# Nine quads by seven products in each last sweep, in turns with plain ones, and side work held one item earlier

## The chip, the core and the metric

The kernel runs on one core of one Trainium2 chip (trn2). The metric is the device time of one launch in microseconds (us), the median of several runs.

## The reference

One layer of a hybrid decoder block on x (256 rows, 2048 columns), all in f32. What touches the change is its second half:

```python
x = x + g1 * (merged @ w_o[l])
h2 = modulate(rms_norm(x, norm2_g[l]), sh2, sc2)
gate, up = jnp.split(h2 @ w_ffn_in[l], 2, axis=-1)
x = x + g2 * ((jax.nn.silu(gate) * up) @ w_ffn_out[l])
return rms_norm(x, final_g)
```

The six modulation rows (shift, scale and gate, twice) are `silu(c) @ ada_w + ada_b`. The hidden width of the FFN is 5632, which is 44 tiles of 128 for `w_ffn_out`.

## The kernel before, in words

**Products in f32.** Each f32 operand is split into a high and a low half. ScalarE (ACT) rounds the high half (`hi`, L330), VectorE (DVE) subtracts it (`lo`, L342), and TensorE (PE) makes a product from three matmuls: high by high, low by high, high by low. Weights stream from memory through SyncE's queue (SP) as tiles `raw` (L313). Half of a weight tile is 512 columns wide, a whole one 1024.

**Items.** The program is a list `items`, one per weight tile. For item i, `step` issues the load of item i+6, the derived tile ("made") of item i+5, the `hi` of item i+4 and the `lo` of item i+3, then what hangs on the item's `before` list, then its matmuls, and it lets the work that waits (posts and sides) into the order of DVE and ACT when a planner's clocks for these engines leave room. The order on every engine is fixed when the program is built.

**Quads by seven products.** A quad is two k tiles (2 x 128) by two column blocks (2 x 512) for two row tiles. A plain quad is two items of 12 matmuls: 8 products of three matmuls. `seven` makes the same from 7 products by sums of weights and of activations (Strassen's scheme in Winograd's form): 21 matmuls in four items. The first item is a half tile (product p, 3 matmuls), the second a whole one (6). The third is `wx`, a difference that GpSimd's queue (POOL) builds by two loads and two adding loads (L443, L447); it gives r and u. The fourth is `wy`, made by DVE from `wx` and two raw tiles (L458, L459); it gives q and the last product. The sums of the activations stand ready as `fs`; ACT rounds them (`ah`, L1404) and DVE subtracts (`al`, L1409), once per seven. The products p, q, r and u of all sevens of a sweep gather in four PSUM banks `pp`, `pq`, `pr`, `pu`, and `combined` (L1425 on) adds them up once at the sweep's end: eleven DVE operations of 512 columns.

**FFN.** `w_ffn_in` is read in eleven slabs. Slab 0 is plain, the others run by `add_pair` with four quads by seven products of eight. `up_f_post` or `gated_rows` transposes the result of a slab (`ft{s}`, two PSUM banks), and `f_parts` makes from it the high and low halves (`fh`, `fl`, L988 and L991) for plain quads, or the sums `fs` for the quads named in `SEVEN` (L1239 to L1249).

**Last sweeps.** `w_ffn_out` runs in two sweeps over k, one for each half of the output columns. The first 36 k tiles are 18 quads, in the order that `TURNS` writes out ("-" plain, "7" by seven products). The last 8 k tiles (the rest) are plain in sweep 1; in sweep 2 they come from two tensors of another layout (f2b, f2c), and behind them stand the products `late`, the last columns of the second row tile. `blocks` adds the residual: `y` (L1461) and `x` (L1463) on DVE, a square on ACT. For sweep 1 this happens at the start of sweep 2, for sweep 2 at the end, and then the final norm (`finish_first`, `finish_last`) scales and stores the rows.

**Side work.** The modulation rows are made by DVE between other work: one operation per column pair, `aw` (L532). `ada_to(m, n)` makes sure that the loads of columns are issued up to a point. `hold_sides` sets the planner's slack so low that no more of them are let in until the second norm (`second_norm`, L1101 on) sets it again.

The lines that the change touches before: `SEVEN` (L68), `TURNS` (L75), `load_rows` (L1048 to L1055) and `hold_sides` with its place (L1087 to L1092). In the changed kernel the lines from L1052 on are numbered two lower, from L1087 on one lower.

Of the kernel before, what the change touches and what calls it, by code (L numbers as in the profile page):

```python
# [64 lines left out]
N_MADE, N_HOLD = 5, 4  # L65

N_SUM = (16, 11)
SEVEN = tuple(range(6, 36, 4))  # L68

SEVEN_1, SLAB_7 = (4, 6, 10, 12), 1  # L70

SLAB_G = 4
TURNS_1 = {1: "---7-77-"}

TURNS = "--7-7-7-7-7-7-7-7-"  # L75
EARLY = NH - 2 * N_HOLD

N_SPARE = 5
# [5 lines left out]
def hybrid_layer(  # L84
# [21 lines left out]
    def b4(name, dt=F32, shape=(4, S)):  # L106
        used["b4"] += 1
        return bp.tile([P, *shape], dt, tag="b4", name=name)
# [6 lines left out]
    def sum_bank(name):  # L115
        return ps.tile([P, 512], F32, tag="bank", name=name)
# [178 lines left out]
    items = []  # L295
# [397 lines left out]
    for i in range(N_PIECES):  # L693
        for n in range(N_F if i == 0 else 0, len(START)):
            s, k0, k1 = START[n], ends[i][n], ends[i + 1][n]
# [8 lines left out]
    def ada_to(*ms):  # L704
        while not {(m, kt) for m in ms for kt in range(NK)} <= cols_done:
            if not ada.advance():
                clock["pe"] += 1
                halves.fetch()
# [339 lines left out]
    def load_rows(s):  # L1048
        def before():
            xr.append(b4(f"xr{s}", F32, (2, 512)))  # L1050
            nc.sync.dma_start(xr[s], x_r[:, s * 512:(s + 1) * 512].rearrange("(t p) n -> p t n", p=P))
            if s == 3:  # L1052
                ada_to(3, 4)
        return before

    def keep_rows(s):
# [29 lines left out]

    def hold_sides():  # L1087

        clock["slack"] = -1e9
        return 0, 0  # L1090

    items[-2].before.append(hold_sides)  # L1092

    def turn(p, of_w=False):

# [132 lines left out]
    def f_parts(s, pts):  # L1228

        seven_ = [j for j in range(2) if 4 * s + 2 * j in SEVEN]  # L1230
        if not seven_:
# [123 lines left out]
    def bank(t, n):  # L1355

        if (t, n) not in fin:
            fin[t, n] = sum_bank(f"pf{t}{n}")
        return fin[t, n]
# [39 lines left out]
    def seven_last(k, n, src):  # L1399
        parts = {}  # L1400

        def parts_high():
            hi = parts[0] = b4(f"ah{n}_{k}", F32R, (8, P))
            nc.scalar.copy(hi[:, 0:7, :], f_sum[k][:, 0:7, :])  # L1404
            return 0, 0.9

        def parts_low():
            lo = parts[1] = b4(f"al{n}_{k}", F32R, (8, P))
            nc.vector.tensor_tensor(lo[:, 0:7, :], f_sum[k][:, 0:7, :], f32(parts[0][:, 0:7, :]), op=ALU.subtract)  # L1409
            return 1.0, 0  # L1410

        def own(to):
            if to not in "pqru":
                return bank(int(to[0]), n + int(to[1]))
            if k == SEVEN[0]:
                fin[to] = sum_bank(f"p{to}{n}")
            return fin[to]

        items[-3].before.append(parts_high)
        items[-2].before.append(parts_low)  # L1420
        seven(
            (src[k], src[k + 1]), lambda j, i: src[k + j][:, i * 512:(i + 1) * 512], True,
            lambda a: [parts[h][:, a, :] for h in range(2)], own, k == SEVEN[0], k == SEVEN[-1],
            (lambda: combined(n)) if k == SEVEN[-1] else None,
        )  # L1425

    def combined(n):

        v = [b4(f"v{n}{i}", F32, (2, 512)) for i in range(2)]
        pq, pqu, pqr, pqur = v[0][:, 0, :], v[0][:, 1, :], v[1][:, 0, :], v[1][:, 1, :]  # L1430
        nc.scalar.copy(pq, fin["p"])

        def add(t, j, x):
            y = sp.tile([P, 512], F32, tag="t2", name=f"yv{n}{t}{j}")
            x2 = x2_of(t, (n + j) * 512, (n + j + 1) * 512)
            nc.vector.tensor_tensor(y, x, g2_of((n + j) * 512, (n + j + 1) * 512), op=ALU.mult)
            nc.vector.tensor_tensor(x2, y, x2, op=ALU.add)

        yield 0, 0.6
        add(0, 0, pq)  # L1440
        nc.vector.tensor_tensor(pq, fin["q"], pq, op=ALU.add)
        yield 1.8, 0
        nc.vector.tensor_tensor(pqu, fin["u"], pq, op=ALU.add)
        nc.vector.tensor_tensor(pqr, fin["r"], pq, op=ALU.subtract)
        nc.vector.tensor_tensor(pqur, fin["r"], pqu, op=ALU.subtract)
        yield 1.8, 0
        add(0, 1, pqr)
        yield 1.2, 0
        add(1, 0, pqu)
        yield 1.2, 0  # L1450
        add(1, 1, pqur)
        free(b4=2)
        yield 1.2, 0
        if n == 2:
            yield from early_rows()
# [38 lines left out]
    for n, src in ((0, w_f2a), (2, w_f2d)):  # L1494
        start = len(items)
        kinds = {"7": iter(SEVEN), "-": iter(k for k in range(0, EARLY, 2) if k not in SEVEN)}
        turns = [next(kinds[c]) for c in TURNS]
        for k in turns + list(range(EARLY, NH if n == 0 else EARLY, 2)):
            if k in SEVEN:
                seven_last(k, n, src)  # L1500
# [244 lines left out]
```

## Time and profile before

| | |
|---|---|
| median of 3 runs | 1537.02 us (1536.7 to 1537.57) |
| profiled execution | 1538.73 us, span 1537.0 us |
| TensorE clock granted | 0.998 |
| PE busy | 1521.0 us, 99% |
| DVE busy | 1365.3 us, 89% |
| ACT busy | 880.7 us, 57% |
| chain that ended last | PE 93%, DMA 3%, DVE 3% |

A row of the timeline gives the start and the length in us, the engine, the line, the operation with out<-in, and the count; in square brackets stands the idle time ahead of it on its engine and what ended it. Rows of one kind that follow each other are drawn together (x3). The spacing of two rows on one engine is a little shorter than the length of the first, since they overlap. "issue" is a wait for nothing that the profile shows.

### The profile page before, as it was taken

How to read it: one execution, taken by the hardware profiler on the slowest of the kernel's cores; microseconds unless marked ns; L12 is line 12 of the kernel's file. 1: busy time of each engine (PE TensorE's matmuls, PEld its weight loads, DVE VectorE, ACT ScalarE, POOL GpSimd, SP SyncE). 2: the span in 40 equal slices, each digit the busy share in tenths (PEclk: the TensorE clock that was granted, in tenths of full speed). 3: DMA queues.
4: the chain of work that ended last, by engine and by line, in shares of the span. 5: the costliest groups of instructions: out<-in, count | busy, mean ns of one | idle time of the engine just before them, and what ended most of it. 6: DMA issues, size and time to landing. Idle time of an engine off the chain costs nothing.

```text
span 1537.0 us, 20204 instructions
## 1 busy us (share of the span) xinstructions
PE 1521.0 (99%) x6851; PEld 1249.0 (81%) x6851; DVE 1365.3 (89%) x1835; ACT 880.7 (57%) x1142; POOL 163.5 (11%) x232
## 2 busy tenths in 40 slices
PE   8999999999999999999999999999999999999997
PEld 5788888888888787888887878888888888888886
DVE  7999999888898888988988899999999999888987
ACT  4654444886964446444444556656665556664664
POOL 0000000000000000000002231034212122321200
PEclk9999999999999999999999999999999999999999
DMA  9999988656786887999999999589898979989983
GB/s 368 383 345 362 345 315 301 207 181 217 241 286 226 291 308 283 364 325 341 377 373 347 312 338 273 167 254 332 274 273 248 269 243 298 288 257 297 275 266 124
DMA packets 138440, 444.58 MB, mean 289 GB/s; under 512 B 16064, under 2 KB 16224, under 8 KB 138336
## 3 DMA queue, kind: packets, MB, share of 16 engines
q1 hardware_dynamic: 113056, 384.02, 70.2%
q0 software_dynamic: 24992, 58.75, 16.1%
q8 instruction: 53, 0.87, 0.2%
q10 hardware_dynamic: 288, 0.52, 0.1%
q14 instruction: 51, 0.42, 0.1%
HBM read 439.02 MB, written 4.21 MB: 288 GB/s over the span
## 4 chain that ended last, share of the span: by engine, by line
PE 93%; DMA 3%; DVE 3%; ACT 0%; issue 0%; SPq 0%; DVEq 0%; ACTq 0%
PE pf L1391 10%; PE f L383 6%; PE f L382 6%; PE f L384 6%; PE wi L383 6%; PE wi L384 6%; PE wi L382 6%; PE wl L384 2%; PE wl L383 2%; PE wga L384 2%; PE wl L382 2%; PE wga L382 2%; PE wgl L383 2%; PE wga L383 2%; PE wgl L384 2%; PE wa L384 2%
## 5 line engine op out<-in xcount | busy, mean ns | idle before, releaser
L330 ACT CAST hi<-raw 128x1024 fp32r<-128x1024 f32 (+1 forms) x540 | 532.3, 996 | 419.1 <-PE wi L384 87.4
L342 DVE TENSOR_TENSOR lo<-raw,hi 128x1024 fp32r<-128x1024 f32 (+1 forms) x540 | 611.9, 1149 | 82.1 <-issue 37.7
L383 PE MATMUL wi<-lo,h 128*128 128x512 f32 x432 | 168.4, 390 | 3.3 <-DVE lo L342 3.3
L382 PE MATMUL wi<-hi,h 128*128 128x512 f32 x432 | 169.9, 393 | 0.0
L384 PE MATMUL wi<-hi,h 128*128 128x512 f32 x432 | 168.2, 389 | 0.0
L382 PE MATMUL f<-hi,h 128*128 128x512 f32 x406 | 158.8, 391 | 0.0
L383 PE MATMUL f<-lo,h 128*128 128x512 f32 x406 | 158.1, 389 | 0.0
L384 PE MATMUL f<-hi,h 128*128 128x512 f32 x406 | 158.0, 389 | 0.0
L532 DVE CUSTOM_DVE_ANT_0 aw<-aw,crow,vec 128x1024 f32<-128x1024 f32 x95 | 120.5, 1277 | 6.0 <-DMA aw<-in_ada_t_dram 6.0
L532 DVE CUSTOM_DVE_ANT_0 aw<-aw,crow,modc 128x1024 f32<-128x1024 f32 x95 | 121.1, 1277 | 1.6 <-DMA aw<-in_ada_t_dram 1.6
L330 ACT CAST hi<-wy 128x1024 fp32r<-128x1024 f32 x55 | 58.0, 1055 | 74.3 <-PE f L384 32.1
L383 PEld LDWEIGHTS wi<-lo,h 128*128 128x128 f32 x432 | 81.1, 188 | 20.9 <-DVE lo L342 4.3
L342 DVE TENSOR_TENSOR lo<-wx,hi 128x1024 fp32r<-128x1024 f32 x55 | 67.2, 1222 | 32.4 <-issue 28.5
L330 ACT CAST hi<-wx 128x1024 fp32r<-128x1024 f32 x55 | 58.0, 1055 | 64.8 <-PE pf L1391 24.0
L382 PEld LDWEIGHTS wi<-hi,h 128*128 128x128 f32 x432 | 81.1, 188 | 16.8 <-ACT acc L611 0.2
L384 PEld LDWEIGHTS wi<-hi,h 128*128 128x128 f32 x432 | 81.1, 188 | 16.7
L384 PEld LDWEIGHTS f<-hi,h 128*128 128x128 f32 x406 | 76.2, 188 | 15.8
L383 PEld LDWEIGHTS f<-lo,h 128*128 128x128 f32 x406 | 76.2, 188 | 15.7 <-DVE lo L342 0.3
L382 PEld LDWEIGHTS f<-hi,h 128*128 128x128 f32 x406 | 76.2, 188 | 15.6
L447 POOL DMA_DIRECT2D wx<-in_w_f_dram x78 | 69.8, 969 | 79.5 <-DMA wx<-in_w_f_dram 78.4
L443 POOL DMA_DIRECT2D wx<-in_w_f_dram x78 | 44.7, 627 | 287.6 <-DVE lo L342 95.2
L342 DVE TENSOR_TENSOR lo<-wy,hi 128x1024 fp32r<-128x1024 f32 x55 | 67.2, 1222 | 6.9 <-ACT hi L330 4.3
(347 smaller groups left out, 3094.1 us busy)
## 6 DMA issues: line engine op xcount, KB each, us to landing
aw<-in_ada_t_dram SPq DMA_DIRECT2D x190, 512.0 KB, 6.7
raw<-in_w_in_dram SPq DMA_DIRECT2D x164, 512.0 KB, 5.1
raw<-in_w_f_dram SPq DMA_DIRECT2D x137, 512.0 KB, 6.5
wx<-in_w_f_dram POOLq DMA_DIRECT2D x156, 256.0 KB, 7.9
raw<-in_w_f2a_dram SPq DMA_DIRECT2D x36, 512.0 KB, 6.4
raw<-in_w_lru_dram SPq DMA_DIRECT2D x32, 512.0 KB, 4.6
raw<-in_w_att_dram SPq DMA_DIRECT2D x32, 512.0 KB, 5.5
raw<-in_w_o_dram SPq DMA_DIRECT2D x32, 512.0 KB, 8.1
```

Source lines behind the costliest of these rows:

```text
L330: nc.scalar.copy(hi[:, cs], live[i][0][:, cs])
L342: nc.vector.tensor_tensor(lo[:, cs], raw[:, cs], f32(hi[:, cs]), op=ALU.subtract)
L382: nc.tensor.matmul(ps, lhsT=lh, rhs=rh, start=start, stop=False, skip_group_check=True)
L383: nc.tensor.matmul(ps, lhsT=lh, rhs=rl, start=False, stop=False, skip_group_check=True)
L384: nc.tensor.matmul(ps, lhsT=ll, rhs=rh, start=False, stop=stop, skip_group_check=True)
L443: nc.gpsimd.dma_start(x[:, j * 512:(j + 1) * 512], block(0, 1))
L447: nc.gpsimd.dma_start(got["x"][:, j * 512:(j + 1) * 512], block(j, j), accum_op=ALU.add)
L532: nc.vector.tensor_tensor_reduce(out=r, in0=r, in1=crow[j], op0=ALU.mult, op1=ALU.add, scale=1.0, scalar=dst if j else vec[:, v:v + 1], ac ...
L1391: nc.tensor.matmul(bank(t, n), lhsT=l[:, rows(t)], rhs=w[:, c0:c0 + 512], start=kt == 0 and k == 0, stop=kt == (EARLY - 2 if (t, n) == (1, ...
```

## The change

Each last sweep gets nine quads by seven products instead of eight: the k tiles 2, 6, ..., 34 instead of 6, 10, ..., 34. The order is now strictly a plain quad, then a seven. Before, it began with two plain quads and ended with a plain one; now it begins with one and ends with a seven. The call `ada_to(3, 4)` moves from the last slab's load of rows to `hold_sides`, and that hangs on the third last item of `w_o` instead of the second last.

```diff
-SEVEN = tuple(range(6, 36, 4))
+SEVEN = tuple(range(2, 36, 4))
-TURNS = "--7-7-7-7-7-7-7-7-"
+TURNS = 9 * "-7"
@@ load_rows
-            if s == 3:
-                ada_to(3, 4)
@@
     def hold_sides():
+        ada_to(3, 4)
         clock["slack"] = -1e9
         return 0, 0
-    items[-2].before.append(hold_sides)
+    items[-3].before.append(hold_sides)
```

Over the whole program PE has 6 matmuls fewer, DVE and ACT make the halves of two more sevens, POOL issues one more `wx` per sweep, and SP issues as many transfers as before. Since k tile 2 belongs to FFN slab 0, that slab's post makes sums `fs` and a shared tile `fc` instead of the halves `fh`, `fl`.

The order of DVE at the start of sweep 1, behind the last operation of the last FFN slab (v1); before:

```order
L1300 TENSOR_TENSOR v1_10_11237<-v1_10_11237,v0_10_11236 128x1024
L342 TENSOR_TENSOR lo532_11290<-raw532_11221,hi532_11261 128x1024
L342 TENSOR_TENSOR lo533_11311<-raw533_11239,hi533_11288 128x1024
L342 TENSOR_TENSOR lo534_11339<-raw534_11259,hi534_11309 128x512
L1409 TENSOR_TENSOR al0_6_11343<-fs11_7918,ah0_6_11313 128x896
L458 TENSOR_TENSOR wy_11363<-wx_11155,raw535_11286 128x512
L459 TENSOR_TENSOR wy_11363<-wy_11363,raw535_11286 128x512
L342 TENSOR_TENSOR lo535_11368<-raw535_11286,hi535_11337 128x1024
L991 TENSOR_TENSOR fl10_11358<-ft10_0_11327,fh10_11357 128x512
L991 TENSOR_TENSOR fl10_11358<-ft10_1_11328,fh10_11357 128x512
```

and now:

```order
L1299 TENSOR_TENSOR v1_10_11241<-v1_10_11241,v0_10_11240 128x1024
L342 TENSOR_TENSOR lo532_11292<-raw532_11228,hi532_11263 128x512
L1408 TENSOR_TENSOR al0_2_11296<-fs01_7536,ah0_2_11267 128x896
L458 TENSOR_TENSOR wy_11317<-wx_11131,raw533_11243 128x512
L459 TENSOR_TENSOR wy_11317<-wy_11317,raw533_11243 128x512
L342 TENSOR_TENSOR lo533_11322<-raw533_11243,hi533_11290 128x1024
L342 TENSOR_TENSOR lo534_11353<-wx_11131,hi534_11320 128x1024
L342 TENSOR_TENSOR lo535_11367<-wy_11317,hi535_11351 128x1024
L991 TENSOR_TENSOR fl10_11360<-ft10_0_11339,fh10_11359 128x512
L991 TENSOR_TENSOR fl10_11360<-ft10_1_11340,fh10_11359 128x512
```

The two `lo` of the second plain quad are gone from here, and the first seven's `lo` of `wx` and `wy` now stand ahead of the two `fl` that read the `ft` banks.

PE in the first seven of sweep 1, from the product r on, with the engines that the row waits for; before, where 24 matmuls of a plain quad and more lie between `ft` and this seven:

```order
L382 MATMUL pr_11415<-hi_11366,ah_6_11313 128x512 [waits Activation_49]
L383 MATMUL pr_11415<-lo_11391,ah_6_11313 128x512 [waits DVE_49]
L384 MATMUL pr_11415<-hi_11366,al_6_11343 128x512
L382 MATMUL pu_11419<-hi_11366,ah_6_11313 128x512 [waits PE_49]
L383 MATMUL pu_11419<-lo_11391,ah_6_11313 128x512
L384 MATMUL pu_11419<-hi_11366,al_6_11343 128x512
L382 MATMUL pq_11429<-hi_11389,ah_6_11313 128x512 [waits Activation_49]
```

and now, where the seven follows the `ft` at once:

```order
L382 MATMUL pr_11383<-hi_11320,ah_2_11267 128x512 [waits Activation_49]
L383 MATMUL pr_11383<-lo_11353,ah_2_11267 128x512 [waits DVE_49]
L384 MATMUL pr_11383<-hi_11320,al_2_11296 128x512
L382 MATMUL pu_11387<-hi_11320,ah_2_11267 128x512 [waits DVE_49,PE_49]
L383 MATMUL pu_11387<-lo_11353,ah_2_11267 128x512
L384 MATMUL pu_11387<-hi_11320,al_2_11296 128x512
L382 MATMUL pq_11397<-hi_11351,ah_2_11267 128x512 [waits DVE_49,PE_49]
```

The first matmuls of `pu` and `pq` now wait for DVE as well: for the two `fl`, which read the banks that `pu` and `pq` take over from `ft10_0` and `ft10_1`.

DVE behind the last seven of sweep 2, from the `lo` of its `wy` on (`v2`, `pq2`, `pu2`, `pr2` and `yv` belong to the combining); before:

```order
L342 TENSOR_TENSOR lo639_13008<-wy_12974,hi639_12995 128x1024
L342 TENSOR_TENSOR lo640_13020<-raw640_12972,hi640_13006 128x1024
L342 TENSOR_TENSOR lo641_13032<-raw641_12993,hi641_13018 128x1024
L342 TENSOR_TENSOR lo642_13047<-raw642_13004,hi642_13030 128x1024
L1436 TENSOR_TENSOR yv200_13061<-v20_13040,g21_12870 128x512
L1437 TENSOR_TENSOR x201_12872<-yv200_13061,x201_12872 128x512
L1441 TENSOR_TENSOR v20_13040<-pq2_12406,v20_13040 128x512
L342 TENSOR_TENSOR lo643_13069<-raw643_13016,hi643_13045 128x1024
L1443 TENSOR_TENSOR v20_13040<-pu2_12396,v20_13040 128x512
L1444 TENSOR_TENSOR v21_13041<-pr2_12392,v20_13040 128x512
L1445 TENSOR_TENSOR v21_13041<-pr2_12392,v20_13040 128x512
L342 TENSOR_TENSOR lo644_13090<-raw644_13028,hi644_13067 128x1024
```

and now:

```order
L342 TENSOR_TENSOR lo645_13082<-wy_13050,hi645_13071 128x1024
L342 TENSOR_TENSOR lo646_13094<-raw646_13048,hi646_13080 128x1024
L342 TENSOR_TENSOR lo647_13106<-raw647_13069,hi647_13092 128x1024
L342 TENSOR_TENSOR lo648_13121<-raw648_13078,hi648_13104 128x1024
L1435 TENSOR_TENSOR yv200_13135<-v20_13114,g21_12918 128x512
L1436 TENSOR_TENSOR x201_12920<-yv200_13135,x201_12920 128x512
L1440 TENSOR_TENSOR v20_13114<-pq2_12391,v20_13114 128x512
L342 TENSOR_TENSOR lo649_13143<-raw649_13090,hi649_13119 128x1024
L342 TENSOR_TENSOR lo650_13161<-raw650_13102,hi650_13141 128x1024
L1442 TENSOR_TENSOR v20_13114<-pu2_12381,v20_13114 128x512
L1443 TENSOR_TENSOR v21_13115<-pr2_12377,v20_13114 128x512
L1444 TENSOR_TENSOR v21_13115<-pr2_12377,v20_13114 128x512
```

The tile behind the seven was that of a plain quad (640, 641) and is now the first of the rest (646); in all 10 `lo` stood between the seven's last one and the end before, and 8 now.

## Rows read from the trace of the kernel before

**Rows 1.** The page, part 1: busy us, share of the span, instructions.

```profile
PE 1521.0 (99%) x6851; PEld 1249.0 (81%) x6851; DVE 1365.3 (89%) x1835; ACT 880.7 (57%) x1142; POOL 163.5 (11%) x232
```

**Rows 2.** Stretches: length; PE, PEld, DVE, ACT, POOL busy us (instructions); clock; DMA share; GB/s.

```profile
1413.40:1500.30 86.90, 86.90 (x385) 71.97 (x384) 78.48 (x82) 57.00 (x67) 11.67 (x16) 1.00 0.81 257
1500.30:1529.10 28.80, 28.77 (x145) 24.85 (x143) 25.76 (x37) 13.30 (x20) 0.00 (x0) 1.00 0.33 113
```

**Rows 3.** Chain of waits, end of sweep 1: start, length in us, what.

```profile
1386.26 38.08 PE pf L1391 x168
```

**Rows 4.** Timeline of PE, first matmuls behind the transpositions before sweep 1.

```profile
1304.40 0.71 PE L1391 MATMUL pf<-hi,fh 128*128 128x512 f32 x2
```

**Rows 5.** Timeline of DVE, start of sweep 1.

```profile
1301.87 2.95 DVE L342 TENSOR_TENSOR lo<-raw,hi 128x1024 fp32r<-128x1024 f32 x3
1304.75 1.08 DVE L1409 TENSOR_TENSOR al<-fs,ah 128x896 fp32r<-128x896 f32 x1
1305.75 0.68 DVE L458 TENSOR_TENSOR wy<-wx,raw 128x512 f32<-128x512 f32 x1
1306.47 0.69 DVE L459 TENSOR_TENSOR wy<-wy,raw 128x512 f32<-128x512 f32 x1
1307.08 1.22 DVE L342 TENSOR_TENSOR lo<-raw,hi 128x1024 fp32r<-128x1024 f32 x1
1308.21 1.28 DVE L991 TENSOR_TENSOR fl<-ft,fh 128x512 fp32r<-128x512 f32 x2
```

**Rows 6.** Timeline of DVE, start of sweep 2.

```profile
1411.91 0.69 DVE L1461 TENSOR_TENSOR y<-pf,g 128x512 f32<-128x512 f32 x1 [0.31 <-PE pf L1391]
1412.63 0.69 DVE L1463 TENSOR_TENSOR x<-y,x 128x512 f32<-128x512 f32 x1
1413.24 1.22 DVE L342 TENSOR_TENSOR lo<-raw,hi 128x1024 fp32r<-128x1024 f32 x1
```

**Rows 7.** Timeline of DVE, from the last seven of sweep 2 to the end.

```profile
1498.05 3.54 DVE L342 TENSOR_TENSOR lo<-raw,hi 128x1024 fp32r<-128x1024 f32 x3
...
1522.01 0.69 DVE L1490 TENSOR_TENSOR x<-x,fg 128x512 f32<-128x512 f32 x1 [0.19 <-ACT y L1470]
...
1523.34 0.69 DVE L1463 TENSOR_TENSOR x<-y,x 128x512 f32<-128x512 f32 x1
...
1529.11 0.29 DVE L1461 TENSOR_TENSOR y<-late,g 128x128 f32<-128x128 f32 x1 [1.30 <-PE late L384]
...
1529.64 0.15 DVE L1563 TENSOR_REDUCE st<-ss 128x1 f32<-128x4 f32 x1
```

**Rows 8.** Timeline of ACT, the last sum of squares but one.

```profile
1528.33 0.19 ACT L1557 ACTIVATION_READ_ACCUMULATOR y<-x 128x1 f32 x1
```

**Rows 9.** Timeline of DVE, ahead of the second norm.

```profile
820.63 1.28 DVE L532 CUSTOM_DVE_ANT_0 aw<-aw,crow,vec 128x1024 f32<-128x1024 f32 x1 [2.02 <-DMA aw<-in_ada_t_dram]
...
823.40 1.23 DVE L342 TENSOR_TENSOR lo<-raw,hi 128x1024 fp32r<-128x1024 f32 x1 [0.34 <-ACT hi L330]
```

**Rows 10.** Timeline of ACT, ahead of the second norm.

```profile
822.32 1.05 ACT L330 CAST hi<-raw 128x1024 fp32r<-128x1024 f32 x1 [3.54 <-DMA raw<-in_w_f_dram]
```

**Rows 11.** Timeline of DVE, first FFN slab with sevens.

```profile
901.09 1.23 DVE L342 TENSOR_TENSOR lo<-raw,hi 128x1024 fp32r<-128x1024 f32 x1 [0.87 <-ACT hi L330]
...
905.37 1.22 DVE L342 TENSOR_TENSOR lo<-wx,hi 128x1024 fp32r<-128x1024 f32 x1
```

**Rows 12.** Timeline of PE, there, the second seven's product r.

```profile
906.75 0.40 PE L383 MATMUL fr<-lo,hs 128*128 128x512 f32 x1
```

**Rows 13.** Timeline of SP's queue, end of sweep 1.

```profile
1380.11 0.38 SPq L313 DMA_DIRECT2D raw<-in_w_f2a_dram  x1
```

**Rows 14.** Timeline of ACT, end of sweep 1.

```profile
1393.38 1.05 ACT L330 CAST hi<-raw 128x1024 fp32r<-128x1024 f32 x1 [5.97 <-DMA raw<-in_w_f2a_dram]
```

**Rows 15.** Timeline of DVE, ahead of the last seven of sweep 1.

```profile
1373.61 3.01 DVE L342 TENSOR_TENSOR lo<-raw,hi 128x1024 fp32r<-128x1024 f32 x3
```

## Prediction, on record before the run

> **What bounds the kernel now.** Read the busy shares first: TensorE (PE) is busy 99% of the span and VectorE (DVE) 89% [rows 1]. The table of stretches then says that no time is lost where the change sits: in the second last sweep PE is busy for 86.90 of 86.90 us and behind it for 28.77 of 28.80, while DVE has 8.4 us to spare in the one and 3.0 in the other [rows 2]. The chain of waits runs through PE without a break, 168 matmuls of a plain stretch in 38.08 us, so one 512-column matmul costs 0.2267 us [rows 3]. A plain quad of 24 is then 5.44 us and a quad by seven products, 21, is 4.76 us. What a matmul saved is worth is therefore 0.2267 us, as long as DVE, which makes the low halves and the sums, keeps ahead of PE. A seven wants more of DVE than a plain quad: beside its lo products the al of the sums, two wy adds and, once per sweep, the combining. So the places to look at are those where a seven comes earlier, or a plain quad goes away, beside other DVE work. About 0.2% (3.07 us) is what a measurement of this kernel can tell from no change.
>
> **Matmuls.** Each last sweep turns one plain quad into a seven: 3 matmuls fewer, 6 in all, 6 x 0.2267 = **-1.36 us**. The additions that come with it (four sums, al, two wy adds, and one pair of GpSimd loads a sweep) sit inside pairs of one plain and one seven as there are eight already in each sweep, and those run without a PE stall [rows 2]: nothing there.
>
> **Start of sweep 1.** The first seven moves from the fourth quad (behind two plain ones and one transposition) to the second, straight behind the transpositions ft of the last FFN slab. In the trace the ft leave PE free at 1304.40 [rows 4]. DVE does three lo from 1301.87, al, two wy, a lo, then the two fl that read the ft banks [rows 5]. In the new order of DVE a short lo, al, wy, wy stand there, and then the lo of the seven's f products; by the spacings of rows 5 (1.00 al; 0.72 and 0.61 wy; 1.13 lo; a lo of 512 as the wy of that size, 0.6) it starts at 1301.87 + 0.6 + 1.00 + 0.72 + 0.61 = 1304.80 and is done 1.22 later, at 1306.02. PE wants it four matmuls behind 1304.40, at 1305.31: a stall of 0.7. Then pu: its bank is the first of ft, and it waits for fl. In the order two more lo stand ahead of fl, which so starts at 1304.80 + 3 x 1.13 = 1308.2 and ends at 1308.9; PE reaches pu twelve matmuls and the 0.7 behind 1304.40, at 1307.85: a stall of 1.1. Together **+1.8 us**; behind it DVE is ahead again for the next seven. Bounds: 0.7 (fl's wait gone) to 2.4 (one lo more ahead of PE). The Trainium skill's "Perfetto Trace Analysis" (Optimizing Tensor Performance, Matmuls) wants independent groups of matmuls to rotate through PSUM banks, so that the reading of one overlaps the next; by that rule pu in a bank of its own would cost 0.7 here instead of 1.8. No row of before shows such a wait: there a plain quad lies between.
>
> **Start of sweep 2.** From 1411.91 DVE carries out the residual adds of sweep 1 (y, x) between the lo products, 0.72 and 0.61 each pair [rows 6]. PE begins the sweep at 1386.26 + 10 x 2.72 = 1413.47 and in the new order reaches the first seven one quad later, at 1418.91; its last low half (of wy) is wanted 16 matmuls on, at 1422.54. The new DVE order puts ahead of that one: four pairs y, x (5.32), a short lo (0.60), al (1.00), two wy (1.33), two lo (2.26), together 10.51, so it starts at 1422.42 and ends 1.22 later, at 1423.64. Stall **+1.1 us**; bounds 0 (a pair of adds slips behind) and 2.4.
>
> **End.** The plain quad behind the last seven of sweep 2 goes, so the combining has 5.44 us less of PE's work to hide in. From 1498.05 to the end of the x at 1523.34 (0.69 long), 25.98 us, DVE is busy all but the 0.19 ahead of 1522.01 [rows 7]. The new order holds the same adds and two lo less (8 for 10), 2.3 us. So against the last seven's end that x, and all that follows it on DVE, comes 2.3 + 0.2 = 2.5 us earlier, while PE's last matmul comes 5.44 earlier. Before, the y at 1529.11 waited 1.30 for PE [rows 7]; now it is DVE that is late, by 5.44 - 2.5 - 1.30 = 1.6. The sum of squares that the reduction behind it needs is read by ScalarE (ACT) at 1528.33 + 0.19 [rows 8], 1.1 ahead of the reduction before; 1.30 of that is gone, so 0.2 to 0.3 more. **+1.9 us**. Bounds 0 (PE still last) and 2.9 (DVE gains nothing for the two lo).
>
> **The hold.** The moved call of the column fetch moves no instruction. Hanging the hold one item earlier takes a single ada column (aw) out of DVE's row ahead of the norm, the one that waited to 820.63 [rows 9]. But the lo ahead of the norm's first multiply starts at 823.40 because ACT's hi waited 3.54 for a weight load until 822.32 [rows 9, 10], and SyncE's order of loads there is the same. So the norm gains **0**; bounds -1.2 (one aw, if that load lands sooner) and 0. The column reappears later: the columns shift by one, and the last now stands in the first FFN pair between a lo of 512 and the lo of wx of the second seven. That lo ended at 906.59 [rows 11] and PE took it up at 906.75 [rows 12]: 0.16 of slack against the 1.28 of an aw [rows 9], so up to 1.1 of stall, 1.2 at the third seven. Against it, one aw less stands a little earlier, and DVE is ahead there; it loses that in a wait of 0.87 for ACT [rows 11], which waits for a load whose slot may now come free sooner. Between 0 and 1.2 I take the middle, **+0.6**.
>
> **Transfer behind sweep 1.** The fetch of the residual rows stands ahead of the same load, that of the third rest item, but PE now comes to it 5.44 us after the last seven and not 10.9. Before, it was issued at 1380.11 [rows 13] and landed at 1393.38 [rows 14], 13.3 us. The new slot is freed by the lo of a plain item, the second of the three from 1373.61 [rows 15], done at 1375.9; with 2 us for issuing the fetch, it goes out at 1377.9. With all of the 13.3 it lands at 1391.2, and is wanted some 2.3 us (a hi, a lo) ahead of 1386.26 + 5.44: 1.9 too late. But two weight loads fewer stand ahead of it in the queue: I take **0**, bounds 0 and 1.9. The combining itself is covered there by eight rest items.
>
> **Sum** against the profiled execution, 1538.73 us (span 1537.0): -1.36 + 1.8 + 1.1 + 1.9 + 0 + 0.6 + 0 = +4.04, so 1542.8; that execution is 1.7 above the median of the runs, 1537.02, so on their scale 1537.02 + 4.04 = **1541.1 us**.
>
> **Rivals.**
> (a) DVE catches up: it takes the adds in the idle time that the stretches show (8.4 us in sweep 2, 3.0 behind it), PE stays last everywhere, and only the matmuls count: 1537.02 - 1.36 = 1535.7. For it: PE was never held in these stretches [rows 2]. Against it: the idle time lies in the middle of the sweep and not at its two ends, and the order on each engine is fixed. It decides at the point where the y at the end still waits for PE. Chance 0.12. The Trainium skill's "Perfetto Trace Analysis" (Identifying the Most-Contended Engine) says to shorten the most-contended engine first; by that rule this is the case that comes. The 99% of rows 1 agree with its choice of PE, the 25.8 of 25.98 us of DVE at the end do not.
> (b) One or two of the four delays fall away, by half the sum: about +2, 1539.0. For it: each is a wait of 0.6 to 1.9 us found by laying rows of before in a new order. Chance 0.18.
> (c) The norm does gain the aw that is taken out of its way: 4.0 - 1.2 = +2.8, 1539.9. Against it the load of 822.32. Chance 0.12.
> (d) The load behind the fetch is late: +1.9, so 1543.0. Against it the shorter queue. Chance 0.08.
> (e) That the hold does not do what it says is already in the forecast: at the norm nothing comes earlier.
>
> **How the numbers follow.** Forecast 0.50, at 1541.1; its own range is 1539.6 to 1542.6 (each stall 0.3 to 0.4 off). Over 3.07 us slower: nine tenths of it, half of (c), and (d): 0.45 + 0.06 + 0.08 = 0.59. Within: the rest of the forecast, (b), half of (c), most of (a): 0.38. Faster by as much would need (a), (c) and 0.5 us more: 0.03. The range reaches from (a), 1535.6, to (d) with a little, 1543.3; left out are several upper bounds at once, and (a) with (c).
>
> **What would show it.** Right: PE gaps of about 0.7 and 1.1 us in the first seven of sweep 1 (the second ahead of pu, released by DVE's fl), 1.1 ahead of a lo of wy in the first seven of sweep 2, and at the end a y on the late bank that no longer waits for PE, with PE's last matmul some 1.6 us ahead of it. The aw gone ahead of the norm, with the lo at the same distance from its load. Wrong: PE busy without a gap in 1298 to 1529; a y that waits for PE; or PE stalled ahead of the third rest item.

## The result, and the profile after

The changed kernel takes 1543.4 us (median of 6 runs, 1541.8 to 1546.81), the kernel before 1536.86 us beside it (6 runs, 1536.09 to 1538.06). The ratio is 1.0044 with a 95% interval of 1.0031 to 1.0057: **6.5 us slower**. The forecast was 1541.1 us, +4.04; the direction was right, the size too small, and the time lies 0.1 us above the range.

The profiled execution took 1543.76 us. Its page, part 1 (busy us, share of the span, instructions), answers to [rows 1]:

```profile
PE 1518.8 (98%) x6845; PEld 1245.7 (81%) x6845; DVE 1373.6 (89%) x1848; ACT 884.7 (57%) x1149; POOL 169.0 (11%) x240
```

PE has 2.2 us less work than before, and the program takes 6.5 us longer. Where PE stood still is in the table of waits of PE (what PE waited with, what released it: us in total, times, longest):

```profile
PE fr L383 <- DVE lo L342: 1.6, 2, 1.4
...
PE pu L382 <- DVE fl L991: 0.8, 1, 0.8
PE f L383 <- DVE lo L342: 0.8, 1, 0.8
PE pq L383 <- DVE lo L342: 0.8, 1, 0.8
...
PE pf L383 <- DVE lo L342: 0.5, 1, 0.5
```

`pf`, `pu` and `pq` belong to the first sevens of the two last sweeps, where the forecast had them. `f` and `fr` are both in the second seven of the first FFN pair (slab 1), where it had one wait of 0.6. The timeline of PE has the same five, with the last matmul of all:

```profile
905.07 0.50 PE L383 MATMUL f<-lo,hs 128*128 128x512 f32 x1 [0.81 <-DVE lo L342]
...
907.41 0.50 PE L383 MATMUL fr<-lo,hs 128*128 128x512 f32 x1 [1.38 <-DVE lo L342]
...
1307.23 0.50 PE L383 MATMUL pf<-lo,ah 128*128 128x512 f32 x1 [0.48 <-DVE lo L342]
...
1310.19 0.47 PE L382 MATMUL pu<-hi,ah 128*128 128x512 f32 x1 [0.83 <-DVE fl L991]
...
1426.15 0.50 PE L383 MATMUL pq<-lo,ah 128*128 128x512 f32 x1 [0.81 <-DVE lo L342]
...
1532.05 0.28 PE L384 MATMUL late<-hi,fl 128*128 128x128 f32 x1
```

The bracket counts from the modelled end of the matmul before. What a wait costs is the distance of the two starts less the 0.2267 of a matmul [rows 3]; it is about 0.16 more, so 1.0 and 1.5 us for the first two, and that is what "wait" means below. The matmul straight behind a wait takes a further 0.1 us, and a dozen behind it about 0.01 each.

The stretches that answer to [rows 2] (length; busy us of PE, PEld, DVE, ACT, POOL; clock; DMA share; GB/s) have PE short of full in sweep 2 and full behind it:

```profile
1417.00:1504.00 87.00, 86.11 (x379) 70.66 (x378) 79.03 (x84) 55.81 (x65) 14.57 (x20) 1.00 0.87 277
1504.00:1532.00 28.00, 28.00 (x142) 24.30 (x142) 26.10 (x35) 13.85 (x20) 0.00 (x0) 1.00 0.24 80
```

At the end DVE, not PE, is late. The timeline of DVE there, against [rows 7]:

```profile
1506.74 3.54 DVE L342 TENSOR_TENSOR lo<-raw,hi 128x1024 fp32r<-128x1024 f32 x3
...
1529.49 0.69 DVE L1462 TENSOR_TENSOR x<-y,x 128x512 f32<-128x512 f32 x1
...
1532.82 0.55 DVE L1460 TENSOR_TENSOR y<-late,g 128x384 f32<-128x384 f32 x1
...
1533.88 0.28 DVE L1460 TENSOR_TENSOR y<-late,g 128x128 f32<-128x128 f32 x1
...
1534.64 0.16 DVE L1562 TENSOR_REDUCE st<-ss 128x1 f32<-128x4 f32 x1 [0.16 <-ACT y L1556]
```

From the first `lo` behind the last seven's to the end of the `x` at 1529.49 DVE is busy 23.44 us without a break (25.98 before, with two `lo` more). The last `y` no longer waits for PE; it starts 1.55 us behind the end of PE's last matmul (1532.05 + 0.28).

**Where the time went.** The kernel before was profiled once more beside the experiments (span 1534.8 us, called "before, second profile" below); the span after is 1542.0, 7.2 longer. Cut at the same instructions of PE:

| stretch | before, second profile | after | difference |
|---|---|---|---|
| start to the transposes ft of slab 0 | 879.88 | 880.54 | +0.66 |
| first FFN pair: from there to the ft of slab 1 | 43.42 | 45.74 | **+2.32** |
| slabs 2 to 10 | 378.16 | 378.51 | +0.35 |
| sweep 1 | 109.69 | 110.95 | **+1.26** |
| sweep 2, to the last matmul | 115.50 | 116.31 | **+0.81** |
| behind the last matmul | 8.15 | 9.95 | **+1.80** |

The first row is within what executions differ by: in six profiles of kernels that are alike up to there it lies between 878.8 and 881.1, and in the first profile of the kernel before it is 882.0. The four in bold make 6.2.

### The profile page after: what moved, and what is told of

The parts are those of the page before. It is cut to its first block, busy times and chain, and to the rows that moved or that the text cites. A ratio compares the mean times of both kernels' runs of the same rounds, so it can differ in the third digit from the quotient of the medians.

```text
span 1542.0 us, 20249 instructions
## 1 busy us (share of the span) xinstructions
PE 1518.8 (98%) x6845; PEld 1245.7 (81%) x6845; DVE 1373.6 (89%) x1848; ACT 884.7 (57%) x1149; POOL 169.0 (11%) x240
## 5 line engine op out<-in xcount | busy, mean ns | idle before, releaser
L1390 PE MATMUL pf<-hi,fc 128*128 128x512 f32 x288 | 79.9, 389 | 0.0
L447 POOL DMA_DIRECT2D wx<-in_w_f_dram x78 | 69.8, 987 | 76.1 <-DMA wx<-in_w_f_dram 75.6
```

Of the source, the lines that this page charges most:

```text
L447: nc.gpsimd.dma_start(got["x"][:, j * 512:(j + 1) * 512], block(j, j), accum_op=ALU.add)
L1390: nc.tensor.matmul(bank(t, n), lhsT=l[:, rows(t)], rhs=w[:, c0:c0 + 512], start=kt == 0 and k == 0, stop=kt == (EARLY - 2 if (t, n) == (1, ...
```

## The experiments

Behind each time stands its ratio to the kernel before, timed beside it (median 1535.9 to 1536.3 us), and, where nothing else is said, the ratio as a difference in us; a single run has none.

### The two halves of the change alone

**The kernel before, once more**, for a second profile. 

> The kernel before, once more, for its trace at the second norm. In the profiled execution of before the granted clock was 0.81 in 826 to 832 us and 0.91 in the 6 us behind, and PE began the FFN 1.0 us later than in the changed kernel, with 0.5 us more in the first matmuls. If this clock loss is particular to that execution (it was 1.87 us above the median of six), the clock here stays at 1.00 in the norm, the FFN's first transpositions come about 1.5 us earlier against the norm's start, and the time is near 1537.0 us. If it belongs to the kernel before, the clock falls again and the hold is what saved it in the changed kernel.

It took 1536.6 us (span 1534.8), 2.1 less than the execution that the forecast was summed on. Its stretches at the second norm (826 on), with the clock as the third number from the right, are the second pair; the first pair is the first profile:

```profile
826.00:832.00 6.00, 4.08 (x22) 3.58 (x21) 4.10 (x10) 3.77 (x10) 1.44 (x3) 0.81 1.06 344
832.00:838.00 6.00, 6.00 (x27) 4.95 (x27) 5.82 (x13) 3.64 (x8) 2.28 (x3) 0.91 1.06 329
```

```profile
826.00:832.00 6.00, 5.69 (x40) 4.82 (x38) 4.13 (x11) 3.47 (x10) 1.06 (x2) 1.00 1.08 320
832.00:838.00 6.00, 6.00 (x30) 4.95 (x29) 5.95 (x12) 4.12 (x8) 3.50 (x4) 1.00 1.03 350
```

In the first profile PE's granted clock had fallen at the norm, behind two waits of PE (1.00 us for DVE's `xr` and 0.92 for ACT's `yo`; the second profile has 0.25 for `yo` alone), and the first slab's first matmul came at 831.86 instead of 830.21. 0.9 of these 1.65 us were there already at the `lo` ahead of the norm, whose weights landed later (823.40 [rows 9], 822.49 in the second profile); 0.7 came behind it. Together they are about the 1.7 us by which that execution stood above its median, and which the forecast took off again.

**The hold alone** (the kernel before with `hold_sides` and `ada_to(3, 4)` as in the change, `SEVEN` and `TURNS` as before).

> Only the hold (and the fetch call in it) moved, the eight sevens as before. DVE's order differs from before by the aw taken out ahead of the norm and the one that comes in ahead of the lo of wx of the second seven in the first FFN pair. Theory A (the aw in the wrong place, as the trace of the changed kernel has it): PE stalls 1 to 1.5 us at that lo and the time is 1.2 to 2.7 us above before, against medians. Theory B (the hold helps the norm by keeping the clock, and pays less than that later): 0 to 0.8 us below before. Theory C (the forecast): +0.6 us.

1539.77 us (11 runs), ratio 1.0024 (1.0015 to 1.0033), +3.7 us. The timelines of DVE and PE at the norm, in the second profile of the kernel before and then with the hold:

```profile
822.49 1.23 DVE L342 TENSOR_TENSOR lo<-raw,hi 128x1024 fp32r<-128x1024 f32 x1 [1.04 <-ACT hi L330]
...
830.21 0.50 PE L382 MATMUL fg<-hi,h 128*128 128x512 f32 x1
```

```profile
822.31 1.23 DVE L342 TENSOR_TENSOR lo<-raw,hi 128x1024 fp32r<-128x1024 f32 x1 [2.27 <-ACT hi L330]
...
830.03 0.50 PE L382 MATMUL fg<-hi,h 128*128 128x512 f32 x1
```

The norm gains nothing: DVE, with an `aw` less, waits longer for the same `hi`, and from that `lo` to the first matmul behind the norm there are 7.72 us in both. When that `hi` gets its weights differs by more from one execution to the next (820.0 to 822.5 in seven profiles without the hold, 820.7 to 822.1 in nine with it). The first FFN pair takes 46.74 us instead of 43.42. So the half that the forecast priced at +0.6 costs 3.3 by the trace, some of it at the lower clock, as shown further on.

**The sevens alone** (`SEVEN` from 2, `TURNS` as `9 * "-7"`, the hold as before).

> Only the ninth seven and the strict turns, the hold as before. From the trace of the changed kernel: sweep 1 +1.3 us, sweep 2 +0.8, the end +1.75, so +3.8 us above before. If the two parts add up, this and the run with the hold alone sum to the changed kernel's +6.5 us (medians). The forecast's own terms: -1.36 + 1.8 + 1.1 + 1.9 = +3.4. If DVE's load earlier in the program (sums instead of low halves in FFN slab 0) costs as well, more than +4.5.

1540.82 us (7 runs), ratio 1.003 (1.0019 to 1.0041), +4.6. The first FFN pair takes 43.37 us. Sweep 1 is 1.27 longer, sweep 2 0.78, the end 1.76: the same as in the changed kernel, so the hold does not change what the sevens cost. These stretches make 3.8 of the 4.6; the rest lies in what executions differ by or is not found. By the ratios the two halves add up to 0.54%, and the change costs 0.44% (0.31 to 0.57). By the stretches they add up to 7.1 us against 6.2: the first FFN pair alone takes 1.0 longer with the hold alone than in the changed kernel.

**Nine sevens between plain ends** (`SEVEN` from 2, the hold as before; the order against that of the changed kernel):

```diff
-TURNS = 9 * "-7"
+TURNS = "--7-77-7-77-7-7-7-"
```

> Nine sevens, the hold as before, but the turns begin with two plain quads and end with a plain one as before, and two pairs of sevens stand side by side: --7-77-7-77-7-7-7-. If the delays of the changed kernel lie at the ends of the sweeps alone, they are gone here and only 6 matmuls less are left: -1.4 us against before (same within the measurement). If two sevens side by side hold PE up (DVE has about 1 us to spare per pair of a plain quad and a seven, and a second seven in place of a plain quad wants about 4 us more of it), each of the four places costs up to 1.5 us: up to +4.6.

1541.62 us (5 runs), ratio 1.0036 (1.0024 to 1.0049), +5.5. Starts and end are free of waits, but a seven straight behind a seven waits for its first `lo` of 1024: 1.0 us three times and 2.1 once. Nine sevens in 18 quads must begin early, end late or stand in pairs, and in these runs each of the three costs more than the 1.36 us of matmuls.

### The sevens: start and end apart

**Eight sevens, the last at the end.**

```diff
-TURNS = "--7-7-7-7-7-7-7-7-"
+TURNS = "--7-7-7-7-7-7-7--7"
```

> The kernel before with its eight sevens, but the last seven of each last sweep moved behind the last plain quad, so that a sweep ends on a seven. No matmul is saved and the sweeps begin as before. By the sum, the end alone is left: VectorE finishes later than PE at the end, +1.75 us (the sevens alone showed that size), all of it behind PE's last matmul, and the transfer behind sweep 1 costs 0. Rival: the end costs nothing by itself and the delays of the sevens are all at the starts: within 0.5 us of the kernel before.

1538.54 us (11 runs), ratio 1.0012 (1.0004 to 1.0021), +1.8. From the last ft to the last matmul it takes 225.18 us (225.19 before), behind it 9.86 (8.15 before): +1.71, all at the end, as the sum had it. The transfer behind sweep 1 costs nothing.

**Eight sevens, the first one a quad earlier.**

```diff
-TURNS = "--7-7-7-7-7-7-7-7-"
+TURNS = "-7-7-7-7-7-7-7-7--"
```

> The kernel before with its eight sevens, but the first one of each last sweep one quad earlier, with a plain quad more at the end. No matmul is saved. By the sum, the two starts alone are left: PE waits of 0.6 and 1.0 us in the first seven of sweep 1 and of 1.2 us in that of sweep 2; against it the end has one plain quad more to hide the combining in, worth nothing as long as PE is last there. +2.8 us in all. Rival: VectorE catches up and the starts cost nothing: within 0.5 us of the kernel before.

1540.98 us (5 runs), ratio 1.0034 (1.0021 to 1.0048), +5.2: more than the 2.8 expected. The waits at the starts are there: the first sevens take 2.0 us (sweep 1) and 1.5 us (sweep 2) more than the 4.76 of 21 matmuls. A further 0.75 stands at the end of sweep 1. The timelines of SP's queue, DVE and PE there:

```profile
1379.51 0.38 SPq L1371 DMA_DIRECT2D g<-gate_d  x1
...
1385.69 0.69 DVE L1436 TENSOR_TENSOR yv<-v,g 128x512 f32<-128x512 f32 x1 [4.31 <-DMA g<-gate_d]
...
1389.42 0.73 PE L1391 MATMUL pf<-lo,fc 128*128 128x512 f32 x2 [0.51 <-DVE lo L342]
```

The combining now begins 5.4 us earlier against the sweep's end, its gate rows are still fetched at their old item, DVE stands 4.31 us at them, and a `lo` behind is late. The forecast's rival (d) was a load that is late behind this fetch. In the changed kernel, where the last seven is nearer to the end, PE does not wait there. One quad the other way the fetch itself is late, for DVE.

**The two fl one place earlier**, on the sevens alone: for slab 10 the `hi` copies and the `fl` are let in together, so that the `fl` stand ahead of the `lo` of `wy`.

> The sevens alone (the hold as before), with the two fl that free the banks of the last transpositions one place earlier in VectorE's row, ahead of the lo of wy of the first seven of sweep 1. The wait of 1.0 us ahead of pu goes. If VectorE's lateness is what counts, it comes back in part ahead of pq's lo product, as 0.5 us, since the lo of wy is now done 1.2 us later: the sweep gains 0.5 us. If the bank is all that counts, no wait follows and the sweep gains 1.0 us. If neither, pu waits as long as before.

One run, 1538.79 us. The timeline of PE in the first seven of sweep 1, first of the sevens alone, then with the `fl` earlier:

```profile
1304.33 0.50 PE L383 MATMUL pf<-lo,ah 128*128 128x512 f32 x1 [0.52 <-DVE lo L342]
1307.29 0.47 PE L382 MATMUL pu<-hi,ah 128*128 128x512 f32 x1 [0.86 <-DVE fl L991]
```

```profile
1302.68 0.50 PE L383 MATMUL pf<-lo,ah 128*128 128x512 f32 x1 [0.52 <-DVE lo L342]
1306.15 0.50 PE L383 MATMUL pq<-lo,ah 128*128 128x512 f32 x1 [0.42 <-DVE lo L342]
```

The wait ahead of `pu` goes and 0.6 of its 1.0 comes back ahead of `pq`. Sweep 1 gains 0.4 us: with DVE a whole `lo` behind, its order mostly trades one wait for another. The other cure, banks of their own for `pu` and `pq` as the Trainium skill's "Perfetto Trace Analysis" (Optimizing Tensor Performance, Matmuls) has it, was not tried.

### The hold: which column costs

With the hold, one `aw` fewer stands ahead of the norm, and from there to the second seven of slab 1 every column is done one place late. The timeline of DVE in the changed kernel:

```profile
900.66 1.23 DVE L342 TENSOR_TENSOR lo<-raw,hi 128x1024 fp32r<-128x1024 f32 x1 [1.40 <-ACT hi L330]
901.80 1.28 DVE L532 CUSTOM_DVE_ANT_0 aw<-aw,crow,modc 128x1024 f32<-128x1024 f32 x1
...
904.34 0.68 DVE L342 TENSOR_TENSOR lo<-raw,hi 128x512 fp32r<-128x512 f32 x1
904.94 1.28 DVE L532 CUSTOM_DVE_ANT_0 aw<-aw,crow,modc 128x1024 f32<-128x1024 f32 x1
...
906.14 1.22 DVE L342 TENSOR_TENSOR lo<-wx,hi 128x1024 fp32r<-128x1024 f32 x1
```

and in the second profile of the kernel before:

```profile
898.92 1.23 DVE L342 TENSOR_TENSOR lo<-raw,hi 128x1024 fp32r<-128x1024 f32 x1 [0.82 <-ACT hi L330]
900.06 1.28 DVE L532 CUSTOM_DVE_ANT_0 aw<-aw,crow,modc 128x1024 f32<-128x1024 f32 x1
...
902.60 0.68 DVE L342 TENSOR_TENSOR lo<-raw,hi 128x512 fp32r<-128x512 f32 x1
903.20 1.22 DVE L342 TENSOR_TENSOR lo<-wx,hi 128x1024 fp32r<-128x1024 f32 x1
```

Two things differ: the `aw` at 904.94 (the forecast's), and the `lo` ahead of both, which against the ft comes 1.1 us later (20.12 us behind them instead of 19.04), because ACT's `hi` and so the weights do. The runs that follow start from the hold alone (the second from the changed kernel) and set at which items columns are let in.

**The column caught up behind the norm.** Two columns at the first item behind the norm, and from there on DVE's row is that of the kernel before.

```diff
+ROWS_AT = {284: 2, 285: 1, 287: 1, 288: 1, 289: 1, 290: 1, 294: 1, 295: 1, 297: 1, 302: 1}
@@ step
-        run_sides(end)
+        if i in ROWS_AT:
+            for _ in range(ROWS_AT[i]):
+                ada.advance(True)
+        elif not 284 <= i <= 302:
+            run_sides(end)
```

> The kernel before with the hold alone, but the one column that the hold takes from ahead of the second norm is done at once behind the norm, and from there on VectorE's row is that of the kernel before. Theory A (the hold costs because the columns stand one place late as far as the first FFN pair): that pair takes 43.4 us as in the kernel before, not the 46.7 of the hold alone, and the time is that of the kernel before, within 0.7 us. Rival (the hold costs by its place alone, or by what the norm leaves behind, wherever the column goes): the pair still takes 45 us or more, and the time is 2 to 4 us above the kernel before.

1536.11 us (11 runs), ratio 1.0001 (0.9992 to 1.0009); the pair takes 43.91 us. With its columns back in place the cost of the hold is gone from the time, and from the pair all but 0.5 us (a wait of 1.1 ahead of `fr` in the first seven).

**The same in the changed kernel** (this edit on top of the change).

> The changed kernel, nine sevens with the hold, but with the column that the hold takes from ahead of the norm done at once behind it, so that the rows of VectorE from there on are those of the sevens alone. If the first FFN pair is all that the hold costs, it takes 43.4 to 43.9 us instead of 45.7, the delays of the sevens stay (1.3 in sweep 1, 0.8 in sweep 2, 1.75 at the end), and the time is 3.9 us above the kernel before by the trace, 4 to 5 by the rounds. If the hold costs elsewhere too, it stays above 5.5.

1540.47 us (6 runs), ratio 1.0032 (1.0021 to 1.0044), +4.6 by the medians (1535.89 beside it); the pair takes 43.58 us. The hold's part of the change ends there, and what is left is the sevens.

**The column of the second seven moved** behind the third seven (no sides at items 303 to 309).

> The hold alone, with one column of the first FFN pair moved: it stood between a short lo and the lo of wx of the second seven, and now stands behind the third seven. No load changes its place. With the hold alone PE waited twice in the second seven, 1.0 us ahead of the f products' lo and 1.5 us ahead of fr's, and then ran at half the clock. Theory A1 (VectorE's column is half of the cost, the weight loads that land later are the other half): the wait ahead of fr falls to about 0.3, the one ahead of f stays at about 1.0, the clock does not fall, the pair takes 44.7 us and the time is 1.3 us above the kernel before. Rival A2 (late loads alone): both waits stay above 0.9, the pair takes 45.5 us or more, and the time stays 2.5 us or more above. Rival A3 (the column alone): both waits go, 43.5 us, the time is that of the kernel before.

1537.28 us (11 runs), ratio 1.0007 (0.9998 to 1.0017); the pair takes 44.64 us. Timeline of PE:

```profile
903.78 0.50 PE L384 MATMUL f<-lo,hs 128*128 128x512 f32 x1 [0.93 <-DVE lo L342]
904.92 0.50 PE L384 MATMUL fr<-lo,hs 128*128 128x512 f32 x1 [0.16 <-DVE lo L342]
```

The wait ahead of `fr` fell from 1.5 to 0.3, that ahead of `f` stayed (1.1): theory A1, to 0.1 us for the pair.

**A column load put ahead of the short weight load** on SP's queue, on top of that.

> The hold alone with the one column moved behind the third seven, as in the run before, and beside that one column load put ahead of the short weight load on SyncE's queue, where it stands in the kernel before. VectorE's row up to the second seven is the same. With the column alone moved, 1.1 us of waiting ahead of the f products of the second seven was left. If the order of the loads is its cause, the weight loads behind go out about 1 us earlier against PE, that wait falls under 0.3 and the first FFN pair takes 43.4 to 43.8 us instead of 44.6. Rival: that wait comes from VectorE's row ahead (a column more between the first and the second seven), and stays at 1 us.

1537.38 us (11 runs), ratio 1.0013 (1.0004 to 1.0022). The loads stand in the order of the kernel before, but the short weight load still leaves 2.3 us ahead of the ft (3.4 there). The wait ahead of `f` is 1.0 still, the pair takes 44.56 us. The expectation failed: the order of the loads alone is not it.

**The column at the end of slab 0 moved by one `lo`**, alone, and then together with the one of the second seven.

> The hold alone, with one column moved back by one place in VectorE's row: the one at the end of the first FFN slab, 6.6 us ahead of the turned ft, which the hold puts ahead of a lo and which stands now behind that lo. The order of the loads is that of the hold alone. If that lo, late by 1.1 us, is what delays the weight loads behind it and so the f products' lo of the second seven, the short weight load goes out some 1.1 us earlier against PE, the wait ahead of f falls from 1.1 to 0.4 us or less, that ahead of fr stays near 1.5, and the first FFN pair takes 45 us (46.7 to 47.5 with the hold alone, part of it at the lower clock). If not, the wait ahead of f stays at 1.0 and the pair takes 45.7 or more.

1538.72 us (11 runs), ratio 1.0014 (1.0005 to 1.0023); the pair takes 46.78 us.

> The hold alone with both columns moved: the one at the end of the first FFN slab behind a lo, and the one in the second seven behind the third seven. If the two columns are the whole cost of the hold, both waits fall to 0.4 us or less, the first FFN pair takes 43.4 to 44.0 us, and the time is that of the kernel before within 0.7 us. If a cost of the hold is left that no column explains, the pair takes 44.6 us as with the second one moved alone, and the time stays 1 us or more above.

1536.57 us (11 runs), ratio 1.0007 (0.9998 to 1.0016); the pair takes 44.02 us. The timelines of PE, of the first and of both:

```profile
903.84 0.50 PE L387 MATMUL f<-lo,hs 128*128 128x512 f32 x1 [0.84 <-DVE lo L343]
906.18 0.50 PE L387 MATMUL fr<-lo,hs 128*128 128x512 f32 x1 [1.36 <-DVE lo L343]
```

```profile
903.33 0.50 PE L387 MATMUL f<-lo,hs 128*128 128x512 f32 x1 [0.33 <-DVE lo L343]
904.46 0.50 PE L387 MATMUL fr<-lo,hs 128*128 128x512 f32 x1 [0.17 <-DVE lo L343]
```

In both the weight load left earlier, as expected (the short one 3.4 us ahead of the ft, 2.3 with the column in its old place), yet the wait ahead of `f` stayed at 1.0 in one execution and was 0.5 in the other, with the same rows of DVE ahead of it. So this column is not shown to be its cause. The weights that the wait ends on land later against the ft in every profile in which the columns of slab 1 are one place late (ACT takes them up 0.6 to 1.2 us later, 2.0 in the last run below), while the DMA engines are busy throughout (share 1.02 to 1.15 in the stretches from 880 to 912, in the second profile of the kernel before too); what delays them stays open.

**The hold alone, once more**, for the clock. 

> The hold alone once more, for one look at the clock. If the two waits of the second seven (2.5 us together) are what lets the granted clock fall, it is again near 0.5 for some 3 us behind them and the first FFN pair takes 46.5 to 47 us; if the fall was of that one execution, the clock is 1.00 there and the pair takes 45.5 us, as in the changed kernel.

One run, 1540.21 us. The pair took 47.50 us; its waits ahead of `f` and `fr` are 1.2 and 1.5, and one of 0.5 stands 8 us ahead of them. Stretches of the hold alone in its first profile, then of this one, then of the changed kernel (clock third from the right):

```profile
904.00:906.00 2.00, 0.97 (x3) 0.49 (x3) 2.00 (x4) 2.00 (x3) 0.62 (x2) 1.00 1.11 206
906.00:908.00 2.00, 1.41 (x3) 1.16 (x4) 2.00 (x3) 0.22 (x1) 0.03 (x1) 0.64 1.12 248
908.00:910.00 2.00, 2.00 (x6) 1.57 (x5) 1.97 (x3) 0.87 (x1) 1.03 (x2) 0.51 1.04 355
```

```profile
906.00:908.00 2.00, 0.76 (x2) 0.66 (x3) 2.00 (x4) 0.87 (x2) 0.00 (x0) 0.73 1.14 208
908.00:910.00 2.00, 2.00 (x7) 1.52 (x6) 2.00 (x3) 0.22 (x1) 1.06 (x2) 0.50 1.05 376
```

```profile
906.00:908.00 2.00, 0.62 (x4) 0.49 (x4) 2.00 (x4) 1.04 (x2) 0.00 (x0) 1.00 1.13 211
908.00:910.00 2.00, 2.00 (x10) 1.68 (x9) 2.00 (x3) 1.06 (x1) 1.07 (x2) 1.00 1.07 315
```

Behind the two waits the hold alone ran some seven matmuls at the lower clock level (1.2 GHz), 0.43 us apart instead of 0.2267, in both executions; the changed kernel, with the same waits, did not in the one that was profiled.

## Why the prediction missed, and what it had right

| term | forecast | measured |
|---|---|---|
| matmuls | -1.36 | in the sweeps' sums |
| start of sweep 1 | +1.8 (0.7 and 1.1) | +1.9 (0.6 and 1.0, the rest in slower matmuls behind them) |
| start of sweep 2 | +1.1 | +1.5 (1.0 ahead of `pq`, 0.2 ahead of `pr`, the rest as above) |
| end | +1.9 | +1.8 |
| norm | 0 | 0 |
| first FFN pair | +0.6 | **+2.3** |
| fetch behind sweep 1 | 0 | 0 |
| sum | +4.04 | +6.2 by the trace, +6.5 by the medians |

- **The matmuls.** Sweeps 1 and 2 are 1.26 and 0.81 longer; with 0.68 of matmuls saved in each that makes 1.9 and 1.5 of delay, and the first sevens take 2.0 and 1.5 more than 21 matmuls do. So the matmuls did save their 0.68, and the delay at each start is larger.
- **Start and end of the sweeps.** Laying the rows of before [rows 4 to 8] in the new order gave each wait to 0.2 us, with its releaser: `pf` by a `lo`, `pu` by `fl`, `pq` by the `lo` of `wy`, and a last `y` 1.55 us behind PE where 1.6 was worked out. Left out were the 0.2 ahead of `pr` and the slower matmuls behind each wait. The run with eight sevens and the last one at the end had the end alone at 1.7.
- **The hold at the norm.** Right, and for the reason given: the `aw` is gone and the `lo` still comes when its weights do [rows 9, 10]; it waits 2.27 us for them with the hold alone.
- **The fetch behind sweep 1.** Right in size. SP issued the load behind the fetch at 1384.61, 9.4 us ahead of the end of the last seven (8.4 was worked out); ACT took its tile up at 1396.27, 11.7 us later (13.3 before), and the `lo` was done 1.3 us before PE wanted it.
- **The step that failed** is "Between 0 and 1.2 I take the middle, +0.6". It had the right column in the right place, and its upper bound was that column's whole price: with the column moved away the wait ahead of `fr` is 1.2 us less. The other half of the step was wrong in sign. The forecast let DVE's wait for ACT [rows 11] shrink since "a slot may now come free sooner"; it grew to 1.40, the weights landed 1.1 us later against the ft, and a second wait of 1.0 stood ahead of the first. What delays these weights no run here shows. With the hold alone the lower clock comes on top. The upper bound of that term was thus too low: in place of 0 to 1.2 the runs show 2.3 in the changed kernel and 3.3 and 4.1 with the hold alone.
- **The rivals.** (a) fell: DVE does not catch up. The Trainium skill's "Perfetto Trace Analysis" (Identifying the Most-Contended Engine) has the engine with the highest occupancy optimized first, and the headroom of TensorE judged by its floating-point work and by how busy its weight loads are. The prediction set the 99% of PE's matmuls beside that rule; the weight loads' share in rows 1 is 81%, below DVE's 89%, so the rule did not clearly choose PE, and 6 matmuls fewer there came with 6.5 us more. The Trainium skill's "Perfetto Trace Analysis" (Optimization Strategy) says to find the gaps of an engine within a regime and what blocks it there. The trace agrees that this is where to look: every wait of the changed kernel in the table above is released by DVE. (b) fell, no delay went away. (c) fell at the norm. (d) did not come here, but a fetch of the same group was late in the run with the first seven earlier.

No kernel tried here is faster than the one before: the hold with its columns caught up is the same (1.0001), all others are slower or not distinguishable from it.

## What to carry to other kernels

An operation taken out of one place of a fixed order is put in at another: follow it to where the old order is met again, and price each operation that has changed neighbours on the way, its loads too, not the two ends alone. A matmul saved is worth nothing at a place where the engine that feeds PE is behind; here those places are the first and the last unit of a sweep, and a seven straight behind a seven. The waits at the first and the last unit could be worked out to 0.2 us each from the old rows in the new order. Where waits come close together, add the lower clock behind them to the upper bound; here that was 1.4 to 1.6 us.

## What had not been expected of the hardware

Two waits of 1.0 to 1.2 and 1.5 us with three matmuls between them were followed by some 3 us at the 1.2 GHz level in three of the four profiles that have them (the hold alone twice, the first column moved alone), and not in the fourth, the changed kernel's. By the spacing of the matmuls it cost 1.4 to 1.6 us where it came; the pair with the hold alone is 1.0 longer than the changed kernel's (46.74 and 45.74). At the norm the first profile of the kernel before fell to 0.81 and 0.91 with two idle times of 1.0 and 0.9 us there; the nine sevens between plain ends have 0.6 and 1.0 there and stayed at 1.00. The Trainium skill's "Perfetto Trace Analysis" (Matmul Optimizations) wants matmuls back-to-back in batches, since the engine scales power with its use; three of the four agree, and the fourth adds that the same pauses don't always have that price. Which side an execution falls on no run here explains.
